# Dense transposed products: both parts of x side by side as one moving tile of 512 columns, units of 256 features, halves added where a unit is read

## The chip, the cores and the metric

The kernel runs on one core of one Trainium2 chip, as one program. The metric is the device time of one execution in microseconds (us). Before the change three runs took 1867.28, 1867.89 and 1869.36 us, with 1867.89 as the median.

## What is computed

The reference is one decoder layer over 256 tokens with 2048 features, in float32:

```python
u = x @ w_in                        # 10544 columns: RWKV-7 | mLSTM | merge gates
y_r = _rwkv7_mixer(u_r, ...)        # 16 heads of 64, a scan over 256 tokens
y_m = _mlstm_mixer(u_m, ...)        # 8 heads, in chunks of 128 tokens
g_r, g_m = _split(u_g + b_gate, [d, d])
mix = (sigmoid(g_r) * (y_r @ w_br) + sigmoid(g_m) * (y_m @ w_bm)) @ w_out
x = _layer_norm(ALPHA * x + mix, ln1_w, ln1_b)
moe = _hier_moe(x, ...)             # top 1 of 4 groups, top 2 of 8 experts, 32 experts of 512
x = _layer_norm(ALPHA * x + moe + sigmoid(x @ w_pg) * (p @ w_ple), ln2_w, ln2_b)
```

The change touches the products with w_in, w_br and w_bm, which are here called the dense products. The product with w_out, the router, the experts and the second norm keep their instructions.

## The kernel before, in words

**Two parts for each number.** The matmuls of the dense products take their operands in a rounded 32-bit format (fp32r in the profile). To keep the precision, every operand is held as a high part (the rounded copy) and a low part (what the rounding left). A product is then three matmuls: high weight by high x, high weight by low x, and low weight by high x. For x the parts are the tiles `xh` and `xl`, each with 16 blocks (k) of 128 features by 256 tokens. For the weights they are made on the fly by `split` (line 198): ScalarE copies 512 columns into `wh` (line 205) and VectorE subtracts that from the raw weight into `wl` (line 206).

**Units and sub-steps.** `unit` (line 178) notes one product with up to 512 output features. A unit of kind "T" leaves features on partitions and tokens along the free axis, one of kind "N" leaves tokens on partitions. A unit has 16 sub-steps (8 for w_br and w_bm), one for each k. A DMA brings the weights of two sub-steps (`issue`, line 186), into one of four raw buffers, and `split` runs at most three sub-steps ahead of the matmuls, in four buffers.

**A "T" sub-step** has four chunks of 128 features. Each chunk takes three matmuls of 256 columns (lines 271 to 273), which add up in one half of a PSUM bank, so a sub-step is 12 matmuls, each with its own load of 128 weight columns. **An "N" sub-step** (lines 278 to 280) has two blocks of tokens with three matmuls each, whose moving operand is a weight tile of 512 columns. A unit's result takes two PSUM banks, and there are two such pairs.

**Reading a unit.** When its last sub-step is issued, the unit's reader (an `evac_...` generator) is put in a list, and `advance`, called once in each sub-step, takes one step of it. For the mixers' inputs the reader scales the PSUM chunk on ScalarE and adds the shifted chunk on VectorE (`shift_mix`); for the gates it is a sigmoid on ScalarE straight from PSUM (line 859); for w_br and w_bm it is a multiplication on VectorE that reads PSUM (lines 870 and 881).

**The mixers** (`rwkv`, four groups of four heads, and `mlstm`) are generators too. After the reader's step, `advance` takes one step of the mixer at hand; a step yields the number of sub-steps until the next. So the matmuls of a mixer stand in TensorE's queue between dense sub-steps, and the dense sub-steps cover the time that VectorE and ScalarE need between two mixer steps. In the five levels of the triangular inverse (lines 517, 520, 527, 378, 532, 534) the steps are one sub-step apart. `while free[...]` locks keep a reader from overwriting what a mixer still needs.

**Order.** lora, r and k of group 0, v of groups 0 and 1, two gate units, r and k of group 1, and so on; then q and k of the mLSTM, its v ("N"), its output gate, w_br, w_bm, w_out ("N"). During w_bm and w_out, hooks on five DMA issues fetch the first expert weights; after w_out, `fetch` fills the other buffers, and the experts run. All engines take their queues in order; the DMAs of weights are issued by SP.

The middle of a "T" sub-step is this:

```python
o = pt_[:, c // 2, (c % 2) * 256:(c % 2) * 256 + 256]
mm(o, h[:, cs_], mh[:, k, :], start=first and c % 2 == 0, stop=False)
mm(o, h[:, cs_], ml[:, k, :], start=False, stop=False)
mm(o, l[:, cs_], mh[:, k, :], start=False, stop=last and (c % 2 == 1 or c == n - 1))
```

Of the kernel before, what the change touches and what calls it, by code (L numbers as in the profile page):

```python
# [43 lines left out]
NCST = _n  # L44

# [62 lines left out]
def hybrid_block(ctx: ExitStack, tc: tile.TileContext, xt, xp, vec, cst, sel8, rows, ln1c, pt, w_lora, w_rkv, w_qk,  # L108
# [41 lines left out]
    xh = _carve(B[8], 0, 16, 256)  # L150
    xl = _carve(B[9], 0, 16, 256)
    wraw = [_carve(B[6], 1024 * i, 2, 512) for i in range(4)]
# [21 lines left out]

    units = []
# [3 lines left out]
    def unit(kind, srcs, nk, ncol, mv, evac):  # L179
        u = len(units)  # L180
        units.append((kind, nk, ncol, mv, evac))
        for k in range(0, nk, 2):
            loads.append([s[:, k:k + 2, :] for s in srcs])
            subs.extend([(u, k, len(loads) - 1), (u, k + 1, len(loads) - 1)])

    def issue(n):
        while state["dma"] < min(n, len(loads)):
            i = state["dma"]
            o = 0
            for s in loads[i]:  # L190
                w = s.shape[-1]
                sp.dma_start(wraw[i % 4][:, :, o:o + w], s)
                o += w
            state["dma"] += 1
            if i in between:
                between[i]()

    def split(n):

        while state["split"] < min(n, len(subs)):  # L200
            i = state["split"]
            u, k, d = subs[i]
            ncol = units[u][2]
            src, h = wraw[d % 4][:, k % 2, :ncol], wh[i % 4][:, :ncol]
            act.activation(h, src, AF.Copy)  # L205
            dve.tensor_tensor(wl[i % 4][:, :ncol], src, h.bitcast(FT), op=OP.subtract)  # L206
            if k % 2 == 1:
                issue(d + 5)
# [40 lines left out]
    def run(hi):  # L249

        i = state["sub"]
        while i < len(subs) and subs[i][0] < hi:
            u, k, _ = subs[i]
            kind, nk, ncol, mv, evac = units[u]
            mh, ml = mv[0] if len(mv) == 1 else mv
# [7 lines left out]
            while mh is yrh and free["y"] < k // 2:  # L263
                advance()
            first, last = k == 0, k == nk - 1
            if kind == "T":
                n = ncol // 128
                for c in range(n):
                    o = pt_[:, c // 2, (c % 2) * 256:(c % 2) * 256 + 256]
                    cs_ = slice(c * 128, c * 128 + 128)  # L270
                    mm(o, h[:, cs_], mh[:, k, :], start=first and c % 2 == 0, stop=False)  # L271
                    mm(o, h[:, cs_], ml[:, k, :], start=False, stop=False)  # L272
                    mm(o, l[:, cs_], mh[:, k, :], start=False, stop=last and (c % 2 == 1 or c == n - 1))  # L273
            else:
                for tb in range(2):
                    o = pt_[:, tb, :]
                    ts_ = slice(tb * 128, tb * 128 + 128)
                    mm(o, mh[:, k, ts_], h, start=first, stop=False)  # L278
                    mm(o, ml[:, k, ts_], h, start=False, stop=False)  # L279
                    mm(o, mh[:, k, ts_], l, start=False, stop=last)  # L280
# [40 lines left out]
    yrh = _carve(B[2], 0, 8, 256)  # L321
    yrl = _carve(B[2], 2048, 8, 256)
    gates = [_carve(B[10], 0, 16, 256), _carve(B[11], 0, 16, 256)]

    free = {"zr": -1, "zv": -1, "Q": -1, "o": -1, "y": -1}

# [4 lines left out]
    def chunk_of(p_, c):  # L331
        return p_[:, c // 2, (c % 2) * 256:(c % 2) * 256 + 256]

# [3 lines left out]
    def evac_lora(p_):  # L337
        mu, omu = vm("mu_l", 0)
        shift_mix(zl, chunk_of(p_, 0), mu, omu)
        mu, omu = vm("mu_l", 1)  # L340
        shift_mix(zg0, chunk_of(p_, 1), mu, omu)
        mu, omu = vm("mu_l", 2)
        shift_mix(zg1, chunk_of(p_, 2)[:32], mu[:32], omu[:32])
        act.activation(igfg, chunk_of(p_, 2), AF.Copy)
        yield
        act.activation(zl[:64], zl[:64], AF.Tanh)
        act.activation(zg0, zg0, AF.Sigmoid)
        act.activation(zg1, zg1, AF.Sigmoid)

    def evac_rk(g):  # L350
        def f(p_):
            while free["zr"] < g - 1:
                yield
            for c in range(2):
                shift_mix(zr[:, c], chunk_of(p_, c), *vm("mu_r", 2 * g + c))
                yield
                shift_mix(zk[:, c], chunk_of(p_, 2 + c), *vm("mu_k", 2 * g + c))
                yield
            if g:
                mixers.append(rwkv(g))  # L360
        return f

    def evac_v(g):
        def f(p_):
            while free["zv"] < g - 1:
                yield
            for c in range(4):
                shift_mix(zv[:, c // 2, c % 2], chunk_of(p_, c), *vm("mu_v", 2 * g + c))
                yield
            if g == 0:  # L370
                mixers.append(rwkv(0))
# [8 lines left out]
    def rwkv(g):  # L380
# [238 lines left out]
        hi, lo_ = yrh[:, 2 * g:2 * g + 2], yrl[:, 2 * g:2 * g + 2]  # L619
# [50 lines left out]
    def evac_qk(w):  # L670
        dst = (qT, kT)[w]

        def f(p_):
            while free["zr"] < 3:
                yield
            for c in range(4):
                src, d, i = chunk_of(p_, c), dst[:, c], 4 * w + c
# [5 lines left out]
            act.activation(sgq, dst, AF.Sigmoid)  # L683
            dve.scalar_tensor_tensor(dst, dst, 1.0 if w == 0 else 0.125, sgq, op0=OP.mult, op1=OP.mult)
# [16 lines left out]
    def evac_o(w):  # L701
        def f(p_):
            for b in range(2):
                act.activation(so[:, 4 * w + 2 * b:4 * w + 2 * b + 2].rearrange("p c t -> p (c t)"), p_[:, b],
                               AF.Sigmoid)
                yield
            free["o"] = w
        return f

    def mlstm():  # L710
        y8 = big(3, FR)
        ymh, yml = _carve(y8, 0, 8, 256), _carve(y8, 2048, 8, 256)
# [1141 lines left out]
```

## Time and profile before

| what | value |
|---|---|
| median of three runs | 1867.89 us |
| the profiled execution's own time | 1869.91 us |
| its span, first to last instruction | 1868.3 us |
| mean granted TensorE clock, share of full speed | 0.944 |
| dense part: first matmul to the last of w_out | 7.3 to about 879 us |
| experts and second norm | the rest |
| TensorE busy in the span | 1658.2 us (89%) |
| VectorE, ScalarE busy | 784.5 us (42%), 585.5 us (31%) |
| bytes moved by DMA | 541.53 MB |

PE is TensorE's matmuls, PEld its weight loads, DVE is VectorE, ACT is ScalarE, POOL is GpSimd and SP is SyncE; L205 is line 205 of the kernel before. A matmul's duration holds its way through the array, so that matmuls overlap in the profile: what a matmul takes from the engine is the distance between two starts. "[0.67 <-ACT B L205]" behind a row says that the engine was idle that long, until that instruction released it.

### The profile page before, as it was taken

The numbers are of one execution on the slowest core, as the hardware profiler recorded it, in microseconds if no ns is written. First come the engines' busy times: TensorE is split into PE (matmuls) and PEld (weight loads), VectorE is DVE, ScalarE is ACT, GpSimd is POOL, SyncE is SP. The second block draws the span as 40 slices with busy tenths as digits, with TensorE's granted clock in tenths as the row PEclk, the third lists the DMA queues.
The fourth block names the chain that finished last, engine by engine and source line by source line (L and its number), as shares of the span: only waits on it lengthen the run. The fifth ranks groups of instructions, "written<-read, shape, count | busy, mean of one in ns | idle before, by whom it ended". The sixth has DMA issues, their size and how long they took to land. (4 is left out here: it accounts for less than half of the span.)

```text
span 1868.3 us, 38467 instructions
## 1 busy us (share of the span) xinstructions
PE 1658.2 (89%) x15819; PEld 1219.8 (65%) x15819; DVE 784.5 (42%) x1621; ACT 585.5 (31%) x1075; POOL 37.2 (2%) x55
## 2 busy tenths in 40 slices
PE   7999999999999999999779978797797878987875
PEld 7999999899988889977326636354374334433332
DVE  4576575664776576855323121221110222321305
ACT  5553643634625564544211100111110111111122
POOL 1000000000000000000000000000000000000002
PEclk9999999999999999999789999999799899988988
DMA  7553343443533436874899999999999999999998
GB/s 238 174 158 115 110 148 102 131 126 101 158 103 121 151 113 196 347 284 161 345 418 413 420 420 421 418 417 421 415 421 421 415 414 394 371 419 407 420 420 345
DMA packets 110632, 541.53 MB, mean 290 GB/s; under 512 B 10476, under 2 KB 37244, under 8 KB 61008
## 3 DMA queue, kind: packets, MB, share of 16 engines
q1 hardware_dynamic: 109696, 537.27, 74.6%
q8 instruction: 152, 2.49, 0.5%
q0 software_dynamic: 720, 1.25, 0.2%
q14 instruction: 64, 0.52, 0.1%
HBM read 536.37 MB, written 2.36 MB: 288 GB/s over the span
## 5 line engine op out<-in xcount | busy, mean ns | idle before, releaser
L271 PE MATMUL dps<-B,B 128*128 128x256 f32 x1456 | 430.2, 295 | 11.1 <-ACT B L205 11.0
L273 PE MATMUL dps<-B,B 128*128 128x256 f32 x1456 | 416.1, 286 | 1.9 <-DVE B L206 1.6
L272 PE MATMUL dps<-B,B 128*128 128x256 f32 x1456 | 415.3, 285 | 0.0
L206 DVE TENSOR_TENSOR B<-B,B 128x512 fp32r<-128x512 f32 (+1 forms) x464 | 313.3, 684 | 194.2 <-ACT B L205 186.2
L205 ACT ACTIVATE B<-B 128x512 fp32r<-128x512 f32 (+1 forms) x464 | 284.8, 623 | 289.7 <-PE dps L272 185.4
L1348 PE MATMUL dps<-B,B 128*32 128x256 f32 x3968 | 266.0, 424 | 89.3 <-DMA B<-in_w_up_dram 69.2
L271 PEld LDWEIGHTS dps<-B,B 128*128 128x128 f32 x1456 | 282.1, 194 | 27.0 <-ACT B L205 12.3
L1348 PEld LDWEIGHTS dps<-B,B 128*32 128x32 f32 x3968 | 146.5, 121 | 213.0 <-issue 130.3
L273 PEld LDWEIGHTS dps<-B,B 128*128 128x128 f32 x1456 | 282.2, 194 | 4.1 <-DVE B L206 3.8
L272 PEld LDWEIGHTS dps<-B,B 128*128 128x128 f32 x1456 | 282.5, 194 | 2.2 <-issue 1.9
L1354 DVE TENSOR_TENSOR M<-M,dps 128x128 f32<-128x128 f32 x31 | 8.9, 288 | 408.1 <-ACT M L1353 408.1
L1369 PE MATMUL mps<-B,M 128*32 128x512 f32 x992 | 126.0, 645 | 8.4 <-issue 3.3
L1712 ACT ACTIVATE B<-mps 32x512 f32<-32x512 f32 x120 | 70.5, 588 | 193.4 <-PE mps L1369 192.3
L1163 PE MATMUL mps<-B,B 128*128 128x206 f32 (+1 forms) x640 | 112.7, 336 | 0.3 <-DVE B L1152 0.3
L1163 PEld LDWEIGHTS mps<-B,B 128*128 128x128 f32 x640 | 110.6, 190 | 1.0 <-DVE B L1152 0.6
L1353 ACT ACTIVATE M<-dps 128x128 f32<-128x128 f32 x31 | 8.6, 277 | 308.3 <-PE dps L1348 308.3
L1369 PEld LDWEIGHTS mps<-B,M 128*32 128x32 f32 x992 | 30.7, 117 | 85.9 <-issue 75.2
L278 PE MATMUL dps<-B,B 128*128 128x512 f32 x192 | 76.6, 399 | 0.0
L280 PE MATMUL dps<-B,B 128*128 128x512 f32 x192 | 75.0, 391 | 0.0
L279 PE MATMUL dps<-B,B 128*128 128x512 f32 x192 | 74.8, 390 | 0.0
L1420 DVE TENSOR_TENSOR B<-mps,V 128x512 f32<-128x512 f32 x31 | 21.4, 692 | 96.1 <-PE mps L1416 96.1
L1389 PE MATMUL mps<-B 128*128 128x512 f32 (+1 forms) x128 | 56.7, 596 | 0.7 <-ACT B L1712 0.7
(478 smaller groups left out, 1660.7 us busy)
## 6 DMA issues: line engine op xcount, KB each, us to landing
B<-in_w_gate_dram SPq DMA_DIRECT2D x124, 1024.0 KB, 14.8
B<-in_w_up_dram SPq DMA_DIRECT2D x124, 1024.0 KB, 15.7
B<-in_w_down_dram SPq DMA_DIRECT2D x60, 2048.0 KB, 14.9
B<-in_w_gt_dram SPq DMA_DIRECT2D x64, 512.0 KB, 3.6
B<-in_w_rkv_dram SPq DMA_DIRECT2D x96, 256.0 KB, 3.3
B<-in_w_pg_dram SPq DMA_DIRECT2D x10, 1854.0 KB, 16.7
B<-in_w_out_dram SPq DMA_DIRECT2D x32, 512.0 KB, 3.6
B<-in_w_qk_dram SPq DMA_DIRECT2D x16, 512.0 KB, 3.7
```

Of the source, the lines that this page charges most:

```text
L205: act.activation(h, src, AF.Copy)
L206: dve.tensor_tensor(wl[i % 4][:, :ncol], src, h.bitcast(FT), op=OP.subtract)
L271: mm(o, h[:, cs_], mh[:, k, :], start=first and c % 2 == 0, stop=False)
L272: mm(o, h[:, cs_], ml[:, k, :], start=False, stop=False)
L273: mm(o, l[:, cs_], mh[:, k, :], start=False, stop=last and (c % 2 == 1 or c == n - 1))
L278: mm(o, mh[:, k, ts_], h, start=first, stop=False)
L279: mm(o, ml[:, k, ts_], h, start=False, stop=False)
L280: mm(o, mh[:, k, ts_], l, start=False, stop=last)
L1163: mm(pp[:, tb], x1T[0][:, k, tb * 128:tb * 128 + 128], w[:, k, :n], start=k == 0 and tb == 0, stop=k == 15 and tb == 1)
L1348: mm(pu[32 * j:32 * j + 32].rearrange("p (a f) -> p a f", a=2), xs[:, 4 * q + k, :], w[:, :, k, 128 * j:128 * j + 128], start=q == QS[0] a ...
L1369: mm(pd[32 * j:32 * j + 32, :], hT_[:, 32 * c:32 * c + 32], w[:, c % 2, 512 * j:512 * j + 512], start=c == 0, stop=c == 3)
L1712: act.activation(yq[32 * i:32 * i + 32, 512 * j:512 * j + 512], pd[32 * j:32 * j + 32, :], AF.Copy)
```

## The change

The two parts of x are laid side by side for each k, so that one matmul with a high weight has 512 moving columns: 256 tokens of the high part and 256 of the low part. Its result fills one PSUM bank; the matmul with the low weight adds 256 columns to the first half. The second half of the bank holds the low part's share alone, and a reader begins with `total`, which copies that half on ScalarE into a tile in SBUF and adds the first half on VectorE.

A "T" unit now has 256 features, and a sub-step has two k of them: 8 matmuls, 4 of 512 and 4 of 256 columns. A DMA brings 4 blocks k of 256 features, and `split` still works on 512 columns. The number of sub-steps is as before: 54 "T" units of 8 or 4 sub-steps in place of 27 of 16 or 8. The outputs of the two mixers (`yr`, `ym`) and x (`xm`) have the new layout; `_Two` gives the "N" units of w_out their two parts from separate tiles.

The order of the units is now r, k, v of group 0, then v of group 1, then gates; so the first mixer can begin 9 sub-steps earlier. The gates, q and k, and the mLSTM's output gate apply their function in SBUF, after `total`.

```diff
@@ unit
-        for k in range(0, nk, 2):
-            loads.append([s[:, k:k + 2, :] for s in srcs])
-            subs.extend([(u, k, len(loads) - 1), (u, k + 1, len(loads) - 1)])
+        n = 2 if kind == "T" else 1
+        for k in range(0, nk, 2 * n):
+            loads.append((ncol, srcs[:, k:k + 2 * n, :]))
+            subs.extend([(u, k, len(loads) - 1), (u, k + n, len(loads) - 1)])
@@ run
-                    mm(o, h[:, cs_], mh[:, k, :], start=first and c % 2 == 0, stop=False)
-                    mm(o, h[:, cs_], ml[:, k, :], start=False, stop=False)
-                    mm(o, l[:, cs_], mh[:, k, :], start=False, stop=last and (c % 2 == 1 or c == n - 1))
+                for k in (k, k + 1):
+                    x, o = mv(k), (k % 2) * ncol
+                    for c in range(ncol // 128):
+                        w = slice(o + c * 128, o + c * 128 + 128)
+                        mm(pt_[:, c], h[:, w], x.rearrange("p a t -> p (a t)"), start=k == 0, stop=False)
+                        mm(pt_[:, c, :256], l[:, w], x[:, 0], start=False, stop=k == nk - 1)
@@ new
+    def total(p_, dst=None):
+        dst = tmp[0] if dst is None else dst
+        n = dst.shape[1]
+        act.activation(dst, p_[:, :n, 256:], AF.Copy)
+        dve.tensor_tensor(dst, dst, p_[:, :n, :256], op=OP.add)
+        return dst
@@ evac_gate
-            for c in range(4):
-                i = 4 * u + c
-                act.activation(gates[i // 16][:, i % 16], chunk_of(p_, c), AF.Sigmoid, bias=v_("b_gate", i))
+            t = total(p_, gates[u // 8][:, 2 * u % 16:2 * u % 16 + 2])
+            yield
+            for c in range(2):
+                act.activation(t[:, c], t[:, c], AF.Sigmoid, bias=v_("b_gate", 2 * u + c))
                 yield
@@ evac_bm
-                dve.tensor_tensor(gm, gm, p_[:, b], op=OP.mult)
+            t = total(p_)
+            yield
+            dve.tensor_tensor(gates[1][:, 2 * u:2 * u + 2], gates[1][:, 2 * u:2 * u + 2], t, op=OP.mult)
@@ order of the first units
-    unit("T", [w_lora], 16, 384, xm, evac_lora)
-    u_rk(0)
-    u_v(0)
+    unit("T", w_lora[:, :, :256], 16, 256, of_x, evac_lora(0))
+    unit("T", w_lora[:, :, 256:], 16, 128, of_x, evac_lora(1))
+    u_mixed(0, 0, 1, 2)
+    u_mixed(1, 2)
     u_gt(0, 1)
-    u_rk(1)
+    u_mixed(1, 0, 1)
@@ x is made when it is needed
-    at_step.update({1: lambda: part_x(1), 4: lambda: part_x(2), 8: lambda: part_x(3), 10: vec_ready})
+    at_step.update({1: lambda: part_x(1), 3: lambda: part_x(2), 5: lambda: part_x(3), 6: vec_ready})
```

## Rows read from the trace of the kernel before

**Rows 1.** The page: busy time of TensorE with its share of the span, and from the 40 slices of the span the lines of TensorE (busy tenths) and DMA (busy tenths).
```profile
PE 1658.2 (89%) x15819; PEld 1219.8 (65%) x15819; DVE 784.5 (42%) x1621; ACT 585.5 (31%) x1075; POOL 37.2 (2%) x55
...
PE   7999999999999999999779978797797878987875
...
DMA  7553343443533436874899999999999999999998
```

**Rows 2.** Busy time of each engine by stretch, from us to us: length, then PE, PEld, DVE, ACT and POOL busy us with their instructions, granted clock (1.00 is full), DMA share and GB/s. The stretches are mixers under dense work (300 to 500), w_br (690 to 748), w_bm (748 to 786), w_out (786 to 880) and the experts.
```profile
300.00:500.00 200.00, 197.24 (x1968) 182.93 (x1968) 120.04 (x217) 107.41 (x191) 3.10 (x7) 0.98 0.41 125
...
690.00:748.00 58.00, 57.72 (x472) 56.31 (x471) 36.22 (x58) 32.88 (x61) 0.00 (x0) 1.00 0.60 191
748.00:786.00 38.00, 38.00 (x315) 37.83 (x315) 31.83 (x48) 19.99 (x33) 0.00 (x0) 1.00 0.88 334
786.00:880.00 94.00, 93.26 (x457) 74.90 (x455) 53.72 (x84) 41.66 (x68) 0.00 (x0) 1.00 0.63 225
...
960.00:1868.00 908.00, 741.01 (x7289) 409.98 (x7289) 212.06 (x491) 132.62 (x274) 14.17 (x14) 0.92 0.99 411
```

**Rows 3.** Groups of TensorE's instructions from 0 to 882 us: line, operation, tiles, shape, count, then busy us in sum, mean ns of one, and idle time before them.
```profile
L271 PE MATMUL dps<-B,B 128*128 128x256 f32 x1456 | 430.2, 295 | 11.1 <-ACT B L205 11.0
...
L278 PE MATMUL dps<-B,B 128*128 128x512 f32 x192 | 76.6, 399 | 0.0
```

**Rows 4.** Timeline of TensorE's matmuls in w_br, where no mixer runs: start us, duration. First, second and last of a stretch without a gap; the last starts 127 matmuls after the first.
```profile
719.74 0.28 PE L273 MATMUL dps<-B,B 128*128 128x256 f32 x1
719.86 0.28 PE L271 MATMUL dps<-B,B 128*128 128x256 f32 x1
...
734.98 0.28 PE L271 MATMUL dps<-B,B 128*128 128x256 f32 x1
```

**Rows 5.** The same view in w_out, whose matmuls have 512 columns. The last starts 30 matmuls after the first.
```profile
793.02 0.39 PE L278 MATMUL dps<-B,B 128*128 128x512 f32 x1
793.25 0.39 PE L279 MATMUL dps<-B,B 128*128 128x512 f32 x1
...
799.83 0.39 PE L278 MATMUL dps<-B,B 128*128 128x512 f32 x1
```

**Rows 6.** Waits of TensorE's matmuls from 34 to 882 us: who waited for whom, us in total, times, longest us.
```profile
PE mps L517 <- DVE B L500: 2.9, 1, 2.9
PE dps L271 <- ACT B L205: 2.7, 2, 2.1
PE mps L786 <- DVE B L781: 1.4, 1, 1.4
PE mps L527 <- DVE B L520: 1.1, 2, 0.5
```

**Rows 7.** Groups of ScalarE's and VectorE's instructions from 0 to 882 us, columns as in Rows 3. L923 copies 512 columns out of PSUM, L870 multiplies 512 columns of PSUM into SBUF, L205 and L206 split weights, L859 is the gates' sigmoid.
```profile
L923 ACT ACTIVATE B<-mps 128x512 f32<-128x512 f32 x8 | 4.7, 597 | 13.2 <-PE mps L921 13.2
L870 DVE TENSOR_TENSOR B<-B,dps 128x512 f32<-128x512 f32 x8 | 5.4, 683 | 0.6 <-PE dps L273 0.6
L206 DVE TENSOR_TENSOR B<-B,B 128x512 fp32r<-128x512 f32 (+1 forms) x464 | 313.3, 684 | 194.2 <-ACT B L205 186.2 <-PE dps L279 3.4 <-PE mps L841 1.4
L205 ACT ACTIVATE B<-B 128x512 fp32r<-128x512 f32 (+1 forms) x464 | 284.8, 623 | 289.7 <-PE dps L272 185.4 <-DVE B L206 70.9 <-PE dps L279 11.6
L859 ACT ACT_TABLE_LOAD x9 | 11.5, 1283 | 0.2
```

**Rows 8.** Timeline of TensorE, VectorE and ScalarE in a level of the triangular inverse of `rwkv`: start us, us.
```profile
413.38 0.69 PE L517 MATMUL mps<-B,B 64*64 64x64 f32 x32
414.13 0.76 DVE L520 TENSOR_TENSOR B<-mps,C 128x256 f32<-128x256 f32 x2 [0.78 <-PE mps L517]
...
415.63 0.69 PE L527 MATMUL mps<-B 64*64 64x64 f32 x32
...
416.25 0.48 DVE L329 SCALAR_TENSOR_TENSOR B<-dps,V,B 128x255 f32<-128x255 f32 x1 [0.77 <-ACT B L328]
...
416.83 0.69 DVE L532 TENSOR_TENSOR B<-B,mps 128x512 f32<-128x512 f32 x1
```

**Rows 9.** VectorE in w_bm: two neighbours of its timeline, and the groups of the router's folding from 748 to 786 us.
```profile
774.68 0.67 DVE L881 TENSOR_TENSOR B<-B,dps 128x512 f32<-128x512 f32 x1
775.28 0.68 DVE L206 TENSOR_TENSOR B<-B,B 128x512 fp32r<-128x512 f32 x1
...
L1081 DVE TENSOR_REDUCE R<-R 128x36 f32<-128x576 f32 x2 | 2.4, 1209 | 0.1
L1080 DVE TENSOR_TENSOR R<-R,V 128x576 f32<-128x576 f32 x2 | 1.5, 752 | 0.0
```

**Rows 10.** Timeline of the start: ScalarE's split of the fourth weight load, ScalarE's table load in the reader of the lora unit, and the matmul that came after it.
```profile
17.52 0.52 ACT L205 ACTIVATE B<-B 128x384 fp32r<-128x384 f32 x1 [2.90 <-DMA B<-in_w_lora_dram]
...
34.82 1.28 ACT L347 ACT_TABLE_LOAD   x1
...
37.41 0.39 PE L271 MATMUL dps<-B,B 128*128 128x256 f32 x1 [0.67 <-ACT B L205]
```

**Rows 11.** The way into the experts: busy time from 870 to 880 us (columns as in Rows 2), the first issue of SP after the dense part, and the group of the experts' first matmuls from 880 to 1866 us.
```profile
870.00:880.00 10.00, 9.26 (x41) 7.32 (x39) 3.48 (x6) 2.08 (x4) 0.00 (x0) 1.00 0.00 0
...
879.06 0.33 SPq L965 DMA_DIRECT2D B<-in_w_gate_dram  x1
...
L1348 PE MATMUL dps<-B,B 128*32 128x256 f32 x3968 | 266.0, 424 | 89.3 <-DMA B<-in_w_up_dram 69.2 <-PEq L1716 9.1 <-issue 7.3
```

More of the change, by code (lines that the diff above doesn't have):

```diff
@@ L188, in issue @@
             i = state["dma"]
[L189 to L193, printed above, removed]
+            ncol, src = loads[i]
+            dst = wraw[i % 4][:, :src.shape[1] * ncol].rearrange("p (k n) -> p k n", n=ncol)
+            sp.dma_start(dst, src)
             state["dma"] += 1
@@ L262, in run @@
             h, l = wh[i % 4], wl[i % 4]
-            while mh is yrh and free["y"] < k // 2:
+            while mv is of_y and free["y"] < k // 2:
                 advance()
-            first, last = k == 0, k == nk - 1
+            first, last = k == 0, k + (2 if kind == "T" else 1) == nk
             if kind == "T":
[L267 to L270, printed above, removed]
-                    mm(o, h[:, cs_], mh[:, k, :], start=first and c % 2 == 0, stop=False)
-                    mm(o, h[:, cs_], ml[:, k, :], start=False, stop=False)
-                    mm(o, l[:, cs_], mh[:, k, :], start=False, stop=last and (c % 2 == 1 or c == n - 1))
-            else:
+                for k in (k, k + 1):
[4 more added lines that the diff above has]
+                        mm(pt_[:, c, :256], l[:, w], x[:, 0], start=False, stop=k == nk - 1)
+            else:
+                x = mv(k)
+                mh, ml = x[:, 0], x[:, 1]
                 for tb in range(2):
@@ L350, in evac_rk, with evac_lora @@
[L350 to L352 removed]
+    def evac_lora(u):
+        def f(p_):
+            if u == 0:
+                t = total(p_)
+                yield
+                shift_mix(zl, t[:, 0], *vm("mu_l", 0))
+                shift_mix(zg0, t[:, 1], *vm("mu_l", 1))
+                return
+            total(p_, igfg[:, None, :])
+            mu, omu = vm("mu_l", 2)
+            shift_mix(zg1, igfg[:32], mu[:32], omu[:32])
+            yield
+            act.activation(zl[:64], zl[:64], AF.Tanh)
+            act.activation(zg0, zg0, AF.Sigmoid)
+            act.activation(zg1, zg1, AF.Sigmoid)
+        return f
@@ L353, in f, with evac_mixed @@
+    def evac_mixed(g, w):
+        name, lock, old = (("mu_r", "zr", g - 1), ("mu_k", "zr", g - 1), ("mu_v", "zv", g - 2))[w]
+        dst = (zr, zk, zv[:, g % 2])[w]
+        def f(p_):
+            t = total(p_)
+            yield
+            while free[lock] < old:
                 yield
             for c in range(2):
-                shift_mix(zr[:, c], chunk_of(p_, c), *vm("mu_r", 2 * g + c))
+                shift_mix(dst[:, c], t[:, c], *vm(name, 2 * g + c))
                 yield
-                shift_mix(zk[:, c], chunk_of(p_, 2 + c), *vm("mu_k", 2 * g + c))
@@ L358, in f @@
-                yield
-            if g:
+            if w == (1 if g else 2):
                 mixers.append(rwkv(g))
[L361 to L366, printed above, removed]
-            for c in range(4):
[L368 to L371, printed above, removed]
         return f
@@ L699, in evac_mv, with evac_o @@
         return f
-    def evac_o(w):
+    def evac_o(u):
         def f(p_):
[L703 to L707, printed above, removed]
+            t = total(p_, so[:, 2 * u:2 * u + 2])
+            yield
+            act.activation(t, t, AF.Sigmoid)
+            free["o"] = u
         return f
@@ L825, in mlstm @@
         yield 2
-        while free["o"] < 1:
+        while free["o"] < 3:
             yield 1
@@ L867, in f @@
         def f(p_):
-            for b in range(2):
-                gt = fl(gates[0][:, 4 * u + 2 * b:4 * u + 2 * b + 2])
-                dve.tensor_tensor(gt, gt, p_[:, b], op=OP.mult)
-                yield
+            gt, t = gates[0][:, 2 * u:2 * u + 2], total(p_)
+            yield
+            dve.tensor_tensor(gt, gt, t, op=OP.mult)
         return f
```

146 lines of the change are left out of this document (71 added, 75 removed).

## The prediction, made before the changed kernel was run

> **What bounds the kernel now.** I read the page's engine lines first, then busy time by stretch, then TensorE's groups and its timeline, then the waits. On the page TensorE is busy for 89% of the span, near full in the first 19 slices, while DMA stands between 3 and 5 tenths in most of these and at 8 or 9 from slice 20 on [rows 1]. So there are two halves: a dense half that TensorE sets and an expert half that DMA sets. By stretch, TensorE is busy 197.2 of 200 us under the mixers and all 38 us in w_bm, at a granted clock of 0.98 to 1.00, the higher of its two levels (2.4 GHz); VectorE has 60% and 84% there; the experts run at a DMA share of 0.99 and 411 GB/s [rows 2]. The waits agree: outside the start, the four largest waits of TensorE in the dense half add up to 8.1 us of 850 [rows 6]. What the dense half costs is therefore what its matmuls cost, and the change works on these: 1456 of each of three kinds [rows 3].
>
> **The matmuls.** A duration of 0.28 us overstates them, since they overlap; distances of starts count. In w_br 127 matmuls of 256 columns take 734.98 - 719.74 = 15.24 us, 0.1200 us each [rows 4]. In w_out 30 matmuls of 512 columns take 6.81 us, 0.2270 us each [rows 5]. 256 more columns cost 0.107 us, so some 0.013 us of each matmul doesn't depend on its columns. Both rows are streams in which every matmul has its own weight load, as in the changed kernel. A chunk cost 3 x 0.1200 = 0.3600 us and will cost 0.2270 + 0.1200 = 0.3470 us. The columns streamed stay the same; what goes is one matmul in three with its weight load. 1456 x 0.013 = 18.9 us; the rounding of the starts leaves 18.5 to 19.5. I take **19 us**. The bounds of this term: nothing, if the 0.013 us were no price of a matmul but something the mixed stream keeps; 19.5 at the other end. I take the upper one, since both streams show it to the same size.
>
> The Trainium skill bears on this in "TensorE: Matmul & The Clock Gate", section "Back-to-back issue gap": a matmul at full clock is to cost its columns at 2.4 GHz and about 2.5 ns more. By that the removed matmuls would give 1456 x 0.0025 = 3.6 us (an estimate from that page), and the time would be near 1866. The trace doesn't agree, with 13 ns [rows 4, 5]; the weight load beside each matmul may be the difference.
>
> **The readers.** 54 units now begin with a copy of 512 columns from PSUM on ScalarE and an addition of 512 on VectorE (one of them half as large). By the nearest rows that is 0.60 us and 0.68 us each, so 32 us more on ScalarE and 37 us more on VectorE [rows 7]. Neither is on the path by itself. VectorE sits idle 194 us in the dense half before line 206, nearly all for ScalarE, and ScalarE 290 us before line 205, most of it for TensorE to free a buffer [rows 7]: both already wait for TensorE. Splitting runs three sub-steps (3 x 1.39 us) ahead, which hides a delay of 1.3 us.
>
> What isn't hidden that way is the mixers. `total` is queued ahead of the mixer's step of the same sub-step, and waits for the unit's last matmul; VectorE's work for the mixer stands behind its addition, and TensorE's next mixer matmuls wait for that. The tightest place is a level, with one sub-step between steps. There line 520 ends at 414.13 + 0.76 = 414.89, and TensorE needs it at 415.63: 0.74 us in reserve [rows 8]. With `total` in front, the copy starts with the mixer's matmuls at 413.4, it and the addition take until 414.7, and line 520 ends at about 415.5, while line 527 now comes 0.05 us earlier (a sub-step is 4 x 0.347 = 1.388 us, not 1.44). So even there it just fits. The old readers took such places as well: line 329 sits just ahead of line 532 in the next step, and nothing stops [rows 8]. Counting sub-steps by the steps that each mixer yields, 29 unit ends fall into the four `rwkv` and 4 into the `mlstm`, 33 in all. Bounds: at 1.28 us each, wholly exposed, 42 us; at the other end a gain of 2 us, if the old readers' share of the waits [rows 6] goes. By the row of the level I take 0.06 us each, **2 us lost**.
>
> **w_bm.** Here VectorE is fullest. Two neighbours start 0.60 us apart [rows 9]. A unit of 4 sub-steps now has 4 splits and 4 reader operations, 8 x 0.60 = 4.8 us, and 8 units with the folding's 2.4 + 1.5 us [rows 9] make 42.3 us, against 32 x 1.388 = 44.4 us of TensorE. It still fits. With durations in place of distances (0.68) it would be 47.4 and cost 3 us; nothing at the other end. I take **0.5 us lost**, by the distances.
>
> **The start.** The first unit is now done with x after 8 sub-steps instead of 16, its first four loads are 512 KB instead of 384, and so x and those weights have to come in sooner. The split of the fourth load waited 2.90 us for its DMA before, until 17.52 [rows 10]. 0.5 MB more ahead of it is about 1.3 us at the 411 GB/s that this core reaches [rows 2], but from there only 2 of 8 sub-steps and 8 short ones are left, where 10 of 16 were. The whole lora product needs the same bytes. Against it, the reader of the lora unit did all in two steps, with a table load of 1.28 us behind which the splits came late, and TensorE waited 0.67 us for line 205 [rows 10]; now it is spread over two units. I take **1 us gained**, between 3 lost (twice the later arrival) and 3 gained.
>
> **At nothing.** Loads: as many bytes, half as many issues for r, k and v; the DMA engines are at 0.41 under the mixers [rows 2], so neither they nor SP are near a bound there. The mixers, 9 sub-steps earlier: they finish before w_br either way, and w_br runs without a gap [rows 4]. Table loads of the gates, 9 before [rows 7]: two more or less are hidden by ScalarE's idle time; without that cover 1.28 us each.
>
> **Into the experts.** From 870 to 880 us DMA is at 0.00, and SP issues the next weights at 879.06, as w_out frees its buffers [rows 11]: what the hooks fetch has come in, and the expert half starts when the dense half ends. Its DMA doesn't care when it begins. So a microsecond saved before 879 is one at the end. Sum: -19 + 2 + 0.5 - 1 = -17.5 us. The profiled execution took 1869.91 us (span 1868.3), which gives 1852.4; it lies 2 us above the median, from which 1867.89 - 17.5 = **1850**. TensorE stays the bound of the dense half; next in line is VectorE in w_bm.
>
> **Rivals.**
> *Slower: the halves added late.* One mechanism: VectorE's addition stands in the mixers' chains and TensorE idles at each unit end. Its price is at most 33 x 1.28 = 42 us; the other terms give 19.5, so it eats the gain from 19.5 / 33 = 0.59 us each, at which the time is 1868, and wholly exposed it is 1868 - 19.5 + 42 = 1890. For it: engines take their queues in order, and VectorE was late once already at such a place (2.9 us, line 517 for line 500) [rows 6]. Against it: 0.74 us in reserve at the tightest step [rows 8]. Half of it exposed gives 1869.5. Chance 0.14, split into 0.04 for a part that still leaves it faster (near 1860), 0.04 for about the same, 0.06 for slower.
> *The removed matmul was nearly free.* If a stream that alternates 512 and 256 columns keeps the 13 ns that the third matmul had, the change saves no more than a few us and the readers cost 2: 1864 to 1869. For it: the columns are the same. Against it: both pure streams. The rule of the Trainium skill's page named above comes out at the same place, with a small price of each matmul as its reason. Chance 0.06, two thirds of it the same.
> *The gain doesn't reach the end.* If the first experts wait for weights fetched by the hooks, part of the 17 us stays there. DMA share is 0.88 in w_bm [rows 2], and the first experts' matmuls wait for w_up 69 us in the whole expert half [rows 11]. Half of it kept gives 1859. Against it: the idle DMA before 880. Chance 0.06, all faster.
>
> **How the numbers follow.** The forecast, 1845 to 1857, has 0.74. Its own range is the start (3 either way) and the mixers (from 2 gained to 4 more lost). Two microseconds below it a gain would need stalls that these rows don't show. To hold 8 in 10 the range takes in part of the first and third rivals: 1845 to 1861. Within 0.2% (3.7 us, what a measurement of this kernel can tell from no change) is 1864 to 1872. Faster: 0.74 + 0.04 + 0.02 + 0.06 = 0.86; same 0.04 + 0.04 = 0.08; slower 0.06.
>
> **What would show it.** Right: a start distance of 0.347 us for a pair in w_br; the dense half's last matmul near 861 instead of 878; the experts' length unchanged; VectorE some 37 us busier. Wrong: pairs at 0.357 or more; waits of mixer matmuls for VectorE above 10 us; line 205's successors waiting for DMA at the start for more than 6 us; w_bm longer than 46 us; or a first expert that starts as late as before.

## The result, and the profile after

The changed kernel takes **1856.97 us** (median of 4 runs, 1855.6 to 1862.35) against 1868.42 us for the kernel before in the same comparison: a ratio of 0.9944 with an interval of 0.9924 to 0.9965, 11.5 us faster by the medians. The forecast was 17.5 us. The profiled execution took 1862.35 us (span 1860.7), 5 us above its median, so a second profile of the same kernel (a0, below, span 1852.0) is read beside it wherever a few microseconds matter.

The page of the changed kernel: busy time, and the slices of TensorE and DMA, as in [rows 1].
```profile
PE 1643.2 (88%) x14363; PEld 1136.0 (61%) x14363; DVE 814.5 (44%) x1675; ACT 618.4 (33%) x1133; POOL 37.3 (2%) x55
...
PE   7999999999999999998779778797797878987866
...
DMA  7543433433435336974899999999999999999997
```
TensorE has 1456 matmuls less and is busy 15.0 us less; VectorE has 30.0 us more and ScalarE 32.9 us more.

Busy time by stretch of the changed kernel, columns as in [rows 2]: mixers under dense work, w_br, w_bm, w_out, experts.
```profile
290.00:490.00 200.00, 195.13 (x1587) 161.79 (x1586) 128.14 (x230) 114.16 (x203) 3.10 (x7) 0.98 0.39 126
682.00:733.00 51.00, 48.88 (x271) 40.52 (x270) 35.81 (x59) 33.40 (x62) 0.00 (x0) 1.00 0.52 163
733.00:779.00 46.00, 45.62 (x258) 39.31 (x258) 39.63 (x63) 25.59 (x47) 0.00 (x0) 1.00 0.84 308
779.00:874.00 95.00, 94.09 (x460) 75.44 (x459) 54.75 (x84) 42.27 (x71) 0.00 (x0) 1.00 0.66 234
960.00:1860.70 900.70, 726.35 (x7232) 406.98 (x7220) 205.24 (x481) 131.83 (x272) 14.08 (x14) 0.92 0.99 411
```
Under the mixers TensorE is idle 4.9 of 200 us, where it was 2.8 [rows 2]. The last matmul of w_out starts at 874.16 us (870.15 in a0) instead of 878.87, not at 861.

Timeline of the changed kernel in w_br, as in [rows 4]: start us, duration. The last row starts 32 pairs after the first.
```profile
720.82 0.39 PE L281 MATMUL dps<-B,B 128*128 128x512 f32 x1
721.04 0.28 PE L282 MATMUL dps<-B,B 128*128 128x256 f32 x1
721.16 0.39 PE L281 MATMUL dps<-B,B 128*128 128x512 f32 x1
...
731.91 0.39 PE L281 MATMUL dps<-B,B 128*128 128x512 f32 x1
```
11.09 us for 32 pairs are **0.3466 us** each, the forecast's 0.347. But not everywhere. The same view where the first units run; the last row starts 18 pairs after the first:
```profile
57.80 0.40 PE L281 MATMUL dps<-B,B 128*128 128x512 f32 x1
58.03 0.28 PE L282 MATMUL dps<-B,B 128*128 128x256 f32 x1
...
64.16 0.40 PE L281 MATMUL dps<-B,B 128*128 128x512 f32 x1
```
Here a pair takes 6.36 / 18 = **0.3533 us** on average, without an idle place in between and at full clock. The trace shows three pairs repeating there, of 0.350, 0.361 and 0.349 us.

**Where the dense part's time went.** For every dense matmul I took the distance to the next start less its price in an undisturbed stream (0.1200 us for 256 columns before, 0.2267 for 512 in an "N" unit, 0.3467 for a pair) and summed the rest by place. In us, the mean of two profiles for the kernel before and for the changed one, single profiles for experiments that are told of below:

| | before | changed | e1 | e3 | e4 | e5, f2 | f1 |
|---|---|---|---|---|---|---|---|
| "T" stream at its price | 524.2 | 504.8 | 504.8 | 504.8 | 504.8 | 504.8 | 524.2 |
| longer distance of pairs | 0.0 | 4.2 | 4.1 | 3.7 | 5.4 | 3.6, 5.7 | 0.0 |
| places where TensorE idles | 4.8 | 11.6 | 7.7 | 8.0 | 7.0 | 7.0, 6.2 | 9.3 |
| first two matmuls after a mixer's | 16.0 | 17.0 | 17.4 | 17.2 | 16.8 | 17.1, 16.6 | 15.9 |
| mixers' matmuls with their waits | 183.6 | 184.4 | 188.3 | 185.2 | 181.6 | 184.4, 183.8 | 182.9 |
| stretches at the lower clock | 3.6 | 5.0 | 3.8 | 6.3 | 2.3 | 6.5, 1.5 | 7.1 |
| start, up to 40 us | 8.4 | 7.4 | 6.8 | 6.8 | 7.7 | 7.5, 7.3 | 6.2 |
| last matmul of w_out at | 877.9 | 872.2 | 870.9 | 870.0 | 863.5 | 868.4, 863.8 | 883.4 |
| from there to the end | 989.3 | 984.2 | 987.1 | 981.3 | 984.9 | 986.7, 982.8 | 985.8 |

So the stream gave 19.4 us, as the forecast said, and the dense part kept 6 of them: 4.2 went into the longer distance, 6.8 into places where TensorE idles, about 2 into the mixers and the matmuls behind them, 1.4 into more of the lower clock; the start gave 1 back. Of the last row, 5 us shorter, the forecast had nothing.

By place, of the 4.8 us in which TensorE was idle before, 3.7 lay at the start of the third `rwkv` group. In the changed kernel about 5.0 lie there, and 2.4 at the start of the first group and 1.2 in w_bm, where there were none.

Waits of TensorE's matmuls in the changed kernel from 34 to 872 us, as in [rows 6].
```profile
PE dps L281 <- ACT B L216: 4.6, 4, 2.1
PE dps L282 <- DVE B L217: 2.5, 7, 0.9
PE mps L802 <- DVE B L797: 2.3, 1, 2.3
PE mps L857 <- ACT B L848: 1.1, 2, 0.8
PE mps L540 <- DVE B L533: 0.9, 4, 0.2
```
The tight step of a level (L527 before, L540 now) waits 0.9 us in all, no more than before. The largest wait is that for ScalarE's copy in `split`. Its place is the start of the third `rwkv` group. Timeline of the changed kernel there, ScalarE with the matmuls that stopped:
```profile
340.06 1.28 ACT L876 ACT_TABLE_LOAD   x1
...
341.88 1.28 ACT L430 ACT_TABLE_LOAD   x1
343.18 0.63 ACT L430 ACTIVATE B<-B 128x516 f32<-128x516 f32 x1
343.72 0.61 ACT L216 ACTIVATE B<-B 128x512 fp32r<-128x512 f32 x1
344.35 1.28 ACT L876 ACT_TABLE_LOAD   x1
...
344.38 0.49 PE L281 MATMUL dps<-B,B 128*128 128x512 f32 x1 [1.86 <-ACT B L216]
...
346.17 1.28 ACT L433 ACT_TABLE_LOAD   x1
...
348.00 1.13 ACT L216 ACTIVATE B<-B 128x512 fp32r<-128x512 f32 x2
...
348.67 0.50 PE L281 MATMUL dps<-B,B 128*128 128x512 f32 x1 [2.13 <-ACT B L216]
```
The mixer's steps (square root L427, exponentials L430 and L433) and the gates' sigmoid (L876) take turns, and each turn loads a table. Between 340.06 and 348.00 ScalarE makes one copy for `split`, where TensorE needs one in every 1.39 us; three sub-steps of lead are used up. The same turns stood at this place before (sigmoid L859, exponential L417 between its two loads), with one long stop. Timeline of the kernel before:
```profile
350.47 1.28 ACT L859 ACT_TABLE_LOAD   x1
...
354.72 1.28 ACT L859 ACT_TABLE_LOAD   x1
...
359.01 0.39 PE L271 MATMUL dps<-B,B 128*128 128x256 f32 x1 [2.07 <-ACT B L205]
```
At the start of the first group it is otherwise. The table loads are the same two before (at 95.37 and 97.80 us) and after (82.09 and 84.92), but in the changed kernel the steps of a reader of v stand between them, and only there does TensorE stop.

### The profile page after: what moved, and what is told of

The parts are those of the page before. It is cut to its first block, busy times and chain, and to the rows that moved or that the text cites. A ratio compares the mean times of both kernels' runs of the same rounds, so it can differ in the third digit from the quotient of the medians.

```text
span 1860.7 us, 35487 instructions
## 1 busy us (share of the span) xinstructions
PE 1643.2 (88%) x14363; PEld 1136.0 (61%) x14363; DVE 814.5 (44%) x1675; ACT 618.4 (33%) x1133; POOL 37.3 (2%) x55
## 5 line engine op out<-in xcount | busy, mean ns | idle before, releaser
L281 PE MATMUL dps<-B,B 128*128 128x512 f32 x1456 | 540.8, 411 | 14.9 <-ACT B L216 11.9
L282 PE MATMUL dps<-B,B 128*128 128x256 f32 x1456 | 413.7, 284 | 2.7 <-DVE B L217 2.5
L216 ACT ACTIVATE B<-B 128x512 fp32r<-128x512 f32 (+1 forms) x464 | 283.1, 622 | 229.1 <-PE dps L281 134.7
L1366 PE MATMUL dps<-B,B 128*32 128x256 f32 x3968 | 260.0, 417 | 97.5 <-DMA B<-in_w_up_dram 82.0
L281 PEld LDWEIGHTS dps<-B,B 128*128 128x128 f32 x1456 | 278.1, 191 | 90.9 <-ACT B L216 14.7
L282 PEld LDWEIGHTS dps<-B,B 128*128 128x128 f32 x1456 | 279.9, 192 | 9.3 <-DVE B L217 7.8
L289 PE MATMUL dps<-B,B 128*128 128x512 f32 x192 | 76.3, 397 | 0.0
L291 PE MATMUL dps<-B,B 128*128 128x512 f32 x192 | 75.2, 392 | 0.2
L290 PE MATMUL dps<-B,B 128*128 128x512 f32 x192 | 74.9, 390 | 0.0
L1194 DVE TENSOR_TENSOR C<-C,mps 128x412 f32<-128x412 f32 (+1 forms) x10 | 5.8, 581 | 103.4 <-PE mps L1186 103.4
L1193 ACT ACTIVATE C<-mps 128x412 f32<-128x412 f32 (+1 forms) x10 | 5.1, 511 | 130.8 <-issue 71.9
## 6 DMA issues: line engine op xcount, KB each, us to landing
B<-in_w_gate_dram SPq DMA_DIRECT2D x124, 1024.0 KB, 15.4
```

What stands on the lines that cost most here:

```text
L281: mm(pt_[:, c], h[:, w], x.rearrange("p a t -> p (a t)"), start=k == 0, stop=False)
L282: mm(pt_[:, c, :256], l[:, w], x[:, 0], start=False, stop=k == nk - 1)
L289: mm(o, mh[:, ts_], h, start=first, stop=False)
L290: mm(o, ml[:, ts_], h, start=False, stop=False)
L291: mm(o, mh[:, ts_], l, start=False, stop=last)
L1366: mm(pu[32 * j:32 * j + 32].rearrange("p (a f) -> p a f", a=2), xs[:, 4 * q + k, :], w[:, :, k, 128 * j:128 * j + 128], start=q == QS[0] a ...
```

## The experiments

Each was timed beside the kernel before on its own chip; ratios are to that, with their intervals. Three theories were to be told apart. **T**: the table loads at such places are what costs. **V**: the halves added by VectorE stand in the mixers' chains wherever they fall. **P**: the longer distance of pairs is what costs.

**a0** is the changed kernel once more.

> The changed kernel once more, unchanged, for a second profile and for a time beside the variants on one chip. All theories: 1855 to 1858 us against about 1868 before. Theory P (a pair of matmuls has two stable distances, 0.347 and 0.353 us, and which one holds depends on the last interruption): pairs at both distances again, with 40 to 60% at the longer one. Theory T (ScalarE's table loads): TensorE idles again for some 5 us at the square root and exponentials of the third rwkv group, near 342 to 349 us.

1855.92 us, ratio 0.9945 (0.9924 to 0.9966).

**e1: the mixers of groups 0 and 2 begin two sub-steps later**, so that their steps fall at other steps of the gates.
```diff
 def rwkv(g):
+    if g % 2 == 0:
+        yield 2
```


> Changed kernel with the first and third rwkv group begun two sub-steps later, so that no step of a gate's reader falls between their square root and their exponentials; every instruction is kept. Theory T: two or three table loads of 1.28 us fewer, TensorE's gaps near 342 to 349 us and near 86 to 90 us shrink from 7.5 us to under 2, time 4 to 7 us lower than the changed kernel, about 1851. Theory V (the halves added late stand in the mixers' chains, wherever these begin): no change within 2 us.

1858.14 us, ratio 0.9948 (0.9930 to 0.9966): no gain. The waits say why (e1, from 34 to 870 us):
```profile
PE mps L542 <- DVE B L535: 4.2, 4, 2.4
...
PE dps L281 <- ACT B L216: 0.2, 1, 0.2
```
The wait for `split` is gone, as T says, and a new one has come in a level. Timeline of e1 there:
```profile
512.56 1.52 DVE L699 SCALAR_TENSOR_TENSOR B<-R,V,B 128x255 f32<-128x255 f32 x3
514.00 0.75 DVE L535 TENSOR_TENSOR B<-mps,C 128x256 f32<-128x256 f32 x2
...
514.47 0.97 PE L542 MATMUL mps<-B 64*64 64x64 f32 x29 [2.42 <-DVE B L535]
```
A reader's step of the mLSTM's q and k, three operations in 1.52 us, now stands ahead of the level's L535. That is an old step of the reader and not an addition of halves, so it doesn't speak for V. The shift moved all later steps of these groups and of those behind them.

**e5 and f2: the same shift, taken back before the levels.** f2 is e5 once more, on another chip.
```diff
 def rwkv(g):
+    if g % 2 == 0:
+        yield 2
...
-        yield Y_PRO[7]
+        yield Y_PRO[7] - (g % 2 == 0)
...
-        yield Y_PRO[13]
+        yield Y_PRO[13] - (g % 2 == 0)
```


> Changed kernel with the first and third rwkv group begun two sub-steps later, and the two sub-steps taken back before their ninth and fifteenth prologue step, so that the levels of all four groups stand where they stand in the changed kernel. Theory T: the gaps near 86 to 90 and 338 to 345 us go from 7 us to about 2 as in the first shift, and TensorE's wait for VectorE in the levels stays at 0.9 us (4.2 with the first shift): dense part ends near 865, 1851 us. If the shift only moves the collision to another place again, 1855 to 1858.

> e5 again, on the same chip as the three-matmul form: the first mixer steps of groups 0 and 2 two sub-steps later and these taken back before the levels. If its gain over the changed kernel is real (6 to 7 us, from the table loads' places), 1847 to 1852 and a ratio to before of 0.987 to 0.991; if it was scatter, 1853 to 1858. In the profile TensorE's waits for ScalarE's splits after 34 us stay under 1 us, and those of the level's matmuls for VectorE near 0.9 us.

1848.89 us, ratio 0.9887 (0.9868 to 0.9906), and 1850.44 us, ratio 0.9902 (0.9875 to 0.9930): 5 to 7 us below the changed kernel, twice (7 to 11 when each kernel is set against the kernel before on its own chip, by medians and by ratios). Waits of f2 from 34 to 870 us:
```profile
PE mps L542 <- DVE B L535: 0.9, 4, 0.2
...
PE dps L281 <- ACT B L216: 0.2, 1, 0.2
```
Both waits are at their small values, with the same work. Up to w_out's last matmul e5 and f2 have 35 table loads, the changed kernel 38. The three that are gone are those of the third group's turns; e5 has one load each there for the square root, the exponentials and the sigmoid:
```profile
333.98 1.28 ACT L429 ACT_TABLE_LOAD   x1
...
336.41 1.28 ACT L432 ACT_TABLE_LOAD   x1
...
344.44 1.28 ACT L878 ACT_TABLE_LOAD   x1
```
So the shift saves three loads where they stopped TensorE, and the idle places at the third group's start come to 1.5 us in place of about 5. Of these 5 us 3.7 were there before the change as well. The shift was not tried on the kernel before, so how much of its gain belongs to the change is not shown. The end of the dense part varies: e5's profiled execution took 1856.74 us, 8 above its median, and its dense part ended at 868.37 us where 865 was expected; f2's ended at 863.77. This is the fastest kernel that computes all of the layer.

**e3: the gates without their table.** The gates take the identity in place of the sigmoid; this leaves out their function, so other experts are chosen.
```diff
-                act.activation(t[:, c], t[:, c], AF.Sigmoid, bias=...)
+                act.activation(t[:, c], t[:, c], AF.Identity, bias=...)
```


> Changed kernel whose gates take the identity in place of the sigmoid, which leaves out the gates' function; every instruction and every step of a reader stays, only ScalarE's table for the sigmoid isn't called for there. Its outputs choose other experts, so the end of the dense part in the profile counts, not the time alone. Theory T: seven table loads fewer, the gaps near 338 to 345 us go from 4.6 us to under 1, the dense part ends 4 to 6 us before that of the changed kernel (870.0), near 865. Theory V: gaps stay within 1 us, since copies and additions stay.

1850.43 us, ratio 0.9899 (0.9881 to 0.9917). TensorE's waits for L216 after 34 us fall from 4.6 (3.5 in a0) to 1.0 us, its idle places from 11.6 to 8.0. T gets part of its effect: at the third group 2.0 us of idle places stay, where under 1 was expected. What was to count did not come, since w_out's last matmul starts at 869.95 us, 0.2 before a0's and not 4 to 6; the lower clock cost 6.3 us in this profile. So this run doesn't show that T is worth its 5.5 us, some or all of which can lie in the experts, which are others here.

**e4: no adding of halves.** Readers take the first half from PSUM; the low part of x is left out of all "T" products. (The short lora unit keeps one copy; the diff shows the main part.)
```diff
 def total(p_, dst=None):
-    act.activation(dst, p_[:, :n, 256:], AF.Copy)
-    dve.tensor_tensor(dst, dst, p_[:, :n, :256], op=OP.add)
-    return dst
+    return p_[:, :n, :256]
```


> Changed kernel whose readers take only the first half of a unit's result, straight from PSUM: no copy on ScalarE and no addition on VectorE, and so the share of x's low part is left out of the outputs of the dense products. It prices the 54 additions in place. Forecast's terms: 2 to 3 us lower than the changed kernel (about 1854). Theory V: 8 us lower or more (1849 or less). Theory T: the table loads stay, so the gap near 342 to 349 us stays at 3 us or more.

1850.47 us, ratio 0.9909 (0.9890 to 0.9928). The copies and additions cost **5.5 us** by the medians, not 2; the forecast's number and V's 8 both miss, and 4.0 us of stops stay at the third group, as T says. In the table 4.6 of that is at idle places and 2.8 among the mixers' matmuls: part of V's price is paid at T's place, since the copies also stand in ScalarE's queue there, so the two can't be added.

**e2 and e6: both 512-column matmuls of a k first, then both of 256**, in the changed kernel and in e5.
```diff
 for c in range(ncol // 128):
     w = slice(o + c * 128, o + c * 128 + 128)
     mm(pt_[:, c], h[:, w], ...)
+for c in range(ncol // 128):
+    w = slice(o + c * 128, o + c * 128 + 128)
     mm(pt_[:, c, :256], l[:, w], ...)
```


> Changed kernel with the order of a sub-step's matmuls changed: for each k first the two of 512 columns, then the two of 256, instead of 512, 256, 512, 256. Nothing else. Theory P in the form that alternating sizes is what makes the longer distance: four matmuls take 0.693 us throughout (0.347 a pair), the 4 us of longer distances go, about 1853. If the longer state belongs to the weight load during a matmul of 256 columns instead, it stays or grows: four matmuls at 0.707 us or more, 1857 or slower.

> The second shift together with the 512, 512, 256, 256 order of the matmuls. Theory T and P add up: 5 us from the gaps and 1 to 2 us from the distances, about 1849 to 1850, which would be below both kernels. If they don't add up, 1851 to 1855.

1854.40 us (0.9936, 0.9915 to 0.9956) and 1850.27 us (0.9896, 0.9878 to 0.9914): 1.5 below the changed kernel and 1.4 above e5, neither of which can be told from nothing. Timeline of e2 in w_br; the last row starts 26 fours after the first:
```profile
716.38 0.62 PE L281 MATMUL dps<-B,B 128*128 128x512 f32 x2
...
734.50 0.62 PE L281 MATMUL dps<-B,B 128*128 128x512 f32 x2
```
Four matmuls take 18.12 / 26 = 0.697 us, here and where the first units run, in e6 too: neither 0.693 nor 0.707. In this order a pair has one distance, 0.3485 us, between the two of the alternating order. That costs 1456 x 0.0018 = 2.6 us over the shorter one, in place of 4.2. So P's loss is real but small, and this order takes back less than half of it.

**f1: three matmuls again, all else as changed.**
```diff
-mm(pt_[:, c], h[:, w], x.rearrange("p a t -> p (a t)"), start=k == 0, stop=False)
+mm(pt_[:, c, :256], h[:, w], x[:, 0], start=k == 0, stop=False)
+mm(pt_[:, c, 256:], h[:, w], x[:, 1], start=False, stop=False)
```


> The changed kernel in everything (units of 256, both parts side by side, readers that add the halves) except that the 512-column matmul is two of 256 again, so three matmuls with their own weight loads per chunk and k, 1456 more. Forecast's matmul term with what the traces gave back: a chunk 0.3600 us again in place of 0.3467 or 0.3533, 1456 x 0.0133 less some 4 us, so about 15 slower than the changed kernel, near 1871, slower than the kernel before by the readers' cost. The removed matmul nearly free: within 4 us of the changed kernel, 1856 to 1860. For the expert part: rival K (form of the dense matmuls) expects a granted clock of 0.77 to 0.85 from 50 to 80 us after the dense half, as in the four profiles of 256-column kernels, and DMA under 403 GB/s from 130 to 150 us after it; if the readers or layout set it, 0.94 to 1.00 and 416 to 418, as in the eight paired ones.

1870.01 us, ratio 1.0003 (0.9987 to 1.0019). Timeline of f1 in w_br; the last row starts 117 matmuls after the first:
```profile
719.76 0.28 PE L282 MATMUL dps<-B,B 128*128 128x256 f32 x1
719.88 0.28 PE L283 MATMUL dps<-B,B 128*128 128x256 f32 x1
...
733.80 0.28 PE L282 MATMUL dps<-B,B 128*128 128x256 f32 x1
```
14.04 / 117 = 0.1200 us: the distance is the old one again, and with it goes the whole gain. Making the pair one matmul is worth 14.1 us by the medians, 11 by the two ratios; all the rest of the change (layout, readers, order) comes out at about nothing against the kernel before. In its profile that nothing is a dense part 5.5 us longer, 3.5 of it by the lower clock, and an expert half 3.5 us shorter.

**b0, b1, b2: why is the expert half shorter?** Its instructions are the same, yet from w_out's last matmul to the end it took 989.4 us before and 981 to 987 in the changed kernels. b0 is the kernel before once more; b1 and b2 are it with a dense half made shorter by other means: the low part of the first mixer's output is left out of two or all four units of w_br.
```diff
-mm(o, h[:, cs_], ml[:, k, :], start=False, stop=False)
+if not n_in <= u < n_in + 2:        # + 4 in b2
+    mm(o, h[:, cs_], ml[:, k, :], start=False, stop=False)
```


> The kernel before once more, for a second profile: how far its dense part (7.3 to 878.9 us in the first profile) and its expert part (989 us) vary from one execution to the next. If the dense part repeats within 1 us, what differs between executions of one kernel sits in the experts, whose DMA is the bound there; if it varies by 4 us as in the two profiles of the changed kernel (874.2 and 870.0), it is TensorE's stream.

> The kernel before, with the high weight by low x matmul left out in two of the four units of w_br (64 matmuls of 256 columns fewer, the low part of the first mixer's output is not used there); the dense half should be 64 x 0.120 = 7.7 us shorter and is otherwise the old one. Theory W (when): the experts and second norm, 989.3 us in the two runs of the kernel before and 982 to 987 in the seven changed kernels, depend on when the dense half ends, against something that runs by its own time (the half-clock stretches): then this kernel's are also 982 to 987 and the time falls by 10 to 15. Rival K (kernel): it is the dense half's own form (256-column matmuls before, pairs after) that sets what clock the expert half begins at: then they stay at 989 and the time falls by 7 to 8.

> The same with the matmul left out in all four units of w_br, 128 x 0.120 = 15.4 us less, close to what the changed kernels save in the dense half. W: the expert part is 982 to 987 us, the time 18 to 22 below before. K: the expert part stays at 989 and the time is 15 to 16 below before, near 1853.

b0 took 1867.72 us (one run; 989.1 for the expert half), b1 1865.84 (ratio 0.9986, 0.9972 to 1.0000; 987.7), b2 1856.99 (0.9946, 0.9926 to 0.9966; 985.4). Neither theory's numbers came: 64 and 128 matmuls less were worth 2.5 and 11.4 us (0 to 5 and 6 to 14 by the intervals), not 7.7 and 15.4, so in these neighbours of the kernel before a microsecond less in w_br was not one at the end. Their traces say where part of it went: from 690 to 720 us, where the mLSTM's last steps run under w_br, TensorE is idle for 2.6 of 30 us in b1 and was for 0.3 before, since shorter sub-steps cover less of the mixer's waits. What did separate the kernels is the clock. Busy time and granted clock (third column from the end) from 50 to 80 us after w_out's last matmul, first the kernel before, then b2, f1, and the changed kernel:
```profile
928.90:958.90 30.00, 20.82 (x242) 9.01 (x231) 3.79 (x16) 3.77 (x8) 0.00 (x0) 0.83 1.01 415
```
```profile
918.20:948.20 30.00, 19.81 (x203) 7.84 (x195) 3.79 (x16) 3.97 (x9) 0.00 (x0) 0.77 1.01 419
```
```profile
933.30:963.30 30.00, 20.73 (x223) 9.61 (x217) 3.88 (x17) 4.06 (x9) 0.00 (x0) 0.83 1.01 418
```
```profile
924.20:954.20 30.00, 23.14 (x221) 10.28 (x215) 7.91 (x24) 4.82 (x11) 0.00 (x0) 0.94 1.01 419
```
All five profiles with dense matmuls of 256 columns have 0.77 to 0.85 there, all nine paired ones 0.94 to 1.00; f1, which differs from the changed kernel in that alone, falls with the first. But its expert half took 985.8 us, as long as the paired ones', and its DMA moved 417 GB/s from 130 to 150 us after w_out, where K expected under 403. So the form of the dense matmuls goes with that clock, and the clock doesn't explain the shorter half. Most of the difference lies late in it: from 600 to 900 us after w_out the DMA moved 405 and 407 GB/s in the two profiles of the kernel before and 409 to 417 in the other twelve, and 5 GB/s more at some 410, over 300 us, are about 3.6 us. Why it did stays **open**; two profiles of the changed kernel alone differ by 4.7 us in that half.

## Why the prediction was right, and where it was not

1856.97 lies in the range of 1845 to 1861, and at the upper edge of the likeliest case's own, 1845 to 1857. The sign and the cause were right; several terms were mis-sized, and the sum hides an error.

**The matmuls, -19.** The 0.013 us is a price of the matmul: 0.3466 in w_br, 0.1200 again in f1. The term's step that failed is that the mixed stream has one distance: 4.2 us of the 19.4 went, which is 4.2 / (1456 x 0.0067) = 43% of the pairs at 0.3533. The lower bound, "something the mixed stream keeps", held for that fifth of the term. The rival of the nearly free matmul falls by f1. By an estimate from the 2.5 ns that the Trainium skill gives for a single matmul ("TensorE: Matmul & The Clock Gate", section "Back-to-back issue gap") f1 would have been within 4 us of the changed kernel; it was 11 to 14 us slower, and the measurement decides.

**At nothing: the table loads, "hidden by ScalarE's idle time".** This step failed. ScalarE idles for hundreds of microseconds in sum, but not in the 8 us at the start of the third group, where the prediction's own price of 1.28 us each applied. The rows for it were there before the change: 3.7 us of stops stood at that place, to which the change added about 1.3. The mixers "9 sub-steps earlier" stood at nothing too, and they decide which of the readers' steps fall between the exponentials: the 2.4 us at the first group came with that (1.2 in e1, 0.9 without the additions in e4). e5 and f2, which move the mixers by two sub-steps, take 5 to 7 us off, from old and new stops together. That the mixers "finish before w_br" was misread: [rows 4] begin 30 us into it, and the mLSTM's last 16 transposes ran from 4 to 12 us into it. w_br took 51.6 us in both profiles of the changed kernel, 49.7 before, though its matmuls alone need 1.7 us less.

**The readers, +2.** Measured 5.5 (e4). The row it rests on held: the level's step waits no longer than before. The loss came at places that the row of the level doesn't stand for, so a price of the tightest step of one kind was carried to all 33. The rival built on it was real with an eighth of its full 42 us.

**w_bm, +0.5, and the start, -1.** w_bm took 46.0 us (45.4 in a0) against 46.1 before, where 44.9 was forecast: about 1 us more than the term. The start has 7.4 for 8.4 us in the table, the forecast's 1 us, though single profiles scatter by as much. Its wait moved from a DMA to VectorE's half of x, in the changed kernel:
```profile
14.74 0.50 PE L281 MATMUL dps<-B,B 128*128 128x512 f32 x1 [1.71 <-DVE B L1073]
...
21.94 0.50 PE L281 MATMUL dps<-B,B 128*128 128x512 f32 x1 [1.27 <-DVE B L1073]
```

**Into the experts.** SP's first issue comes as w_out ends, at 874.35 us, 0.2 us after the last matmul started, as at [rows 11]; the rival that the gain stays there falls. "The experts' length unchanged" was wrong, by about 5 us in favour of the forecast: a dense part that kept 6 us and an expert half that gave 5 make the 11 that were measured. Without that unexplained part the time would have been near 1862, still faster but outside the range: that it lies inside is luck.

Of the marks that were named, the pair distance was met in w_br; VectorE came to 30 in place of 37 us, because the page counts overlapping time once: the 54 additions last 36.8 us in sum, and neighbours on VectorE overlap, as in [rows 9]. The last matmul near 861 and the experts' length were missed. None of the marks against it was met, that of w_bm (46 us) by less than 0.1.

## What to carry to other kernels

Fewer and wider matmuls are worth their fixed cost times their number, and that cost is read from starts in two streams of different widths; take off a share for a mixed stream until its own distance is measured. An engine's idle sum is no cover at a place: where a change moves one chain of work against another, list what one in-order queue holds in the few microseconds where they meet, table loads above all. After such a change, moving one chain by a sub-step or two and back is a cheap experiment, and here it gave about half as much again as the change itself, in part from stops that were older than the change.

## What the runs showed of the hardware

An alternating stream of 512 and 256 columns has two steady distances, 0.3467 and 0.3533 us a pair, and holds one over many pairs; pure streams of either width have one (0.1200 and 0.2267 us), and so has the order 512, 512, 256, 256 (0.697 us for the four). The place in the program doesn't choose: w_br ran at 0.3467 in the changed kernel's profile and at 0.3533 in f2's. What does wasn't found.

In stretches of some 3 or 7 us TensorE runs at the lower of its two levels while its stream is full. Timeline and busy time of the changed kernel in one (granted clock 0.50, which is 1.2 GHz); the last matmul starts six pairs after the first:
```profile
189.40 0.63 PE L281 MATMUL dps<-B,B 128*128 128x512 f32 x1
189.83 0.41 PE L282 MATMUL dps<-B,B 128*128 128x256 f32 x1
...
193.24 0.63 PE L281 MATMUL dps<-B,B 128*128 128x512 f32 x1
```
```profile
189.50:191.50 2.00, 2.00 (x8) 1.71 (x8) 1.12 (x5) 1.34 (x4) 0.00 (x0) 0.50 0.00 0
```
A pair takes 3.84 / 6 = 0.640 us, which is 768 columns at 1.2 GHz and nothing more: the fixed cost of a matmul, 0.013 us at the upper level, isn't seen at the lower one. These stretches cost between 1.5 and 7.1 us of a dense part, and are part of why single profiles of one kernel differ by several microseconds. They don't begin just anywhere. Of the 52 in the dense parts of the fourteen profiles 39 begin within 1.1 us of the start of a mixer's matmul, in moments that make up 35% of these parts (the one shown begins at 187.4 us, among matmuls of 64 columns); eight begin behind the third group's stops and five behind stops in the first 21 us. Which of these places is hit differs between executions.
